# All eight output-gate projections moved between the keys and the mLSTM values, with the gate scan beside them

## The chip, the cores and the metric

The kernel runs on one core of a Trainium2 chip. The metric is the device time in microseconds of one execution. Before the change three runs took 955.58, 956.19 and 957.11 us; the median is 956.19 us.

## The reference, cut to what matters

One decoder layer on 512 tokens of width 1024, all in float32. One RMS-normalised input `h` is multiplied by one wide matrix; its column blocks feed a chunkwise mLSTM (4 heads), a sliding-window attention (16 query heads on 4 key heads), and two branch gates. The parts that the change touches:

```
proj = h @ w_in[i]
qk_ml, v_ml, o_ml, if_pre, q_sw, k_sw, v_sw, g_a, g_b = jnp.split(proj, split_idx, axis=-1)
...
gates = (if_pre + b_if[i]).astype(jnp.float32)
ig = gates[..., :ML_HEADS]
lf = jax.nn.log_sigmoid(gates[..., ML_HEADS:])
h_ml = mlstm_chunkwise(q_ml, k_ml, v_ml.reshape(B, S, ML_HEADS, ML_DV), ig, lf)
h_ml = h_ml * lax.rsqrt(jnp.mean(h_ml * h_ml, axis=-1, keepdims=True) + EPS)
y_a = jax.nn.sigmoid(o_ml) * h_ml
y_b = swa_with_sinks(q_sw, k_sw, v_sw, sinks[i])
merged = jax.nn.sigmoid(g_a) * (y_a @ w_branch_a[i]) + jax.nn.sigmoid(g_b) * (y_b @ w_branch_b[i])
```

After that come an output projection, a squared-ReLU MLP, a gated per-layer embedding and a final norm, none of which the change touches.

## The kernel before, in words

Every float32 operand of a matrix product is split into a high part and a low part: ScalarE casts the high part (L134), VectorE subtracts it from the source (L135), and TensorE takes three products per pair (high by high, high by low, low by high). A projection to 128 output channels (`proj_T`, L288) is thus 24 products of 128x128 by 128x512 into one PSUM bank. Its weights come as one 512 KB transfer into a ring of four raw buffers (`wr`), and are split into rings of four buffers (`wh`, `wl`); the cast for a fifth weight waits until TensorE has finished with the first.

PSUM has three tags: `g` (two banks, for projections), `t` (two banks, for transposes and small results; the key projections use it too), `a` (two pairs of banks). Instructions of one engine run in the order in which they stand; that order comes from a scheduler that works when the kernel is built, so it need not be the order of the source.

The stages that matter here, in time:

- Norm, and the projection of the SWA values and the gate pre-activations (`gt`), up to about 31 us.
- The two key projections (L297 to L307). The keys are wanted on both halves of the partitions, so each result is cast and subtracted four times, in half-height pieces of 64x512 (`kk` at L304, `kl` at L305).
- The sums of `h` over token halves (`h_sum`, L326) and their splits (`h_split`, tiles `hS`), which the next two stages use as operands of a Strassen-Winograd scheme (`seven`, L350: seven products in place of eight). VectorE also forms sums of the raw weights in place (L359, L360, L365, L367).
- The mLSTM values (`vml`), 168 products of 512 columns; then the two branch gates (`gate_proj`), whose sigmoids go to DRAM.
- Four of the eight output-gate projections (`o_proj`, L482; sigmoid at L485), written to DRAM through POOL's queue (L491).
- The gate scan (L494 to L537): transposes of `gt`, log-sigmoid by Exp and Ln with their table loads on ScalarE, three kinds of VectorE instructions on four partitions (the scans at L509 and L512 among them), the maxima `em` by another Exp, and 14 little transposes into `gc`.
- SWA: query projections (`q_proj`, each in half-height pieces), scores, softmax, outputs, with the mLSTM's query and key projections in between; then the mLSTM itself with the second branch's projections between.
- The loop over `ya` (L744 to L753): for each of eight blocks four transposes of the normed mLSTM output, a multiply by the norm gain and the output gate (`sy`, L752), and a split into `ya`. The gates of blocks 0 to 3 are read back from DRAM in pairs (`gate_of`, two buffers of the tag `pT`), those of blocks 4 to 7 are projected inside this loop.
- The first branch's projections (L757), which need all eight blocks of `ya`, then the rest of the layer.

SyncE's queue issues all weight loads, in order, each waiting for its buffer.

Of the kernel before, what the change touches and what calls it, by code (L numbers as in the profile page):

```python
# [36 lines left out]
def block_kernel(  # L37
# [29 lines left out]
    nc = tc.nc  # L67
    V, A, G, T = nc.vector, nc.scalar, nc.gpsimd, nc.tensor


    def pool(stack, name, **kw):
        return stack.enter_context(tc.tile_pool(name=name, bufs=1, reuse_waits="tile", **kw))
# [7 lines left out]
    c1 = pool(st_s, "c1", side="right")  # L80
# [5 lines left out]
    def nm(s):  # L86
        n_names[0] += 1
        return f"{s}_{n_names[0]}"


    def ps_g():
        return pp.tile([P, 512], F32, tag="g", bufs=2, name=nm("psg"))

    def ps_t():
        return pp.tile([P, 512], F32, tag="t", bufs=2, name=nm("pst"))
# [9 lines left out]
    def act_f(n="f"):  # L105
        return ap.tile([P, 512], F32, tag="act", bufs=NACT, name=nm(n))
# [21 lines left out]
    def r32(t):  # L128
        return t.bitcast(F32)

    def split(dst, src, scale=None):

        if scale is None:
            A.copy(dst[0], src)  # L134
            V.tensor_sub(dst[1], src, r32(dst[0]))  # L135
        else:
            A.activation(dst[0], src, AF.Copy, scale=scale)
            V.scalar_tensor_tensor(dst[1], src, scale, r32(dst[0]), ALU.mult, ALU.subtract)
# [7 lines left out]
    def load_w(src, n, dims, raw=None):  # L146

        if raw is None:
            raw = load_raw(src, n)
        parts = [wp.tile([P, 1056], F32R, tag=t, bufs=WB, name=nm(t))[:, :n] for t in ("wh", "wl")]  # L150
        split(parts, raw[:, :n])
        return [q.rearrange("p (k c) -> p k c", k=dims) for q in parts]
# [5 lines left out]
    last_mm = [None]  # L158
# [17 lines left out]
    def mm_T(ps, w, acts, first=True, last=True):  # L176

        ops = []
        for k in range(len(acts)):
            ops += pairs([q[:, k, :] for q in w], acts[k])  # L180
        chain(ps, ops, first, last)
# [11 lines left out]
    ident = cp.tile([P, P], F32, name="ident")  # L193
# [5 lines left out]
    zeros4 = c1.tile([4, P], F32, name="zeros4")  # L199
# [10 lines left out]
    sel_f = c1.tile([4, 4, P], F32, name="sel_f")  # L210
# [45 lines left out]
    gt = c1.tile([P, NT, 8], F32, name="gt")  # L256
    h2, hT = big_hl("h")
    hf = []
    for m in range(NT):
# [4 lines left out]
        for c in range(2):  # L264
            o = slice(c * 512, (c + 1) * 512)
# [4 lines left out]
        for kq in range(2):  # L270
            ps = ps_t()
# [8 lines left out]
        ps = ps_g()  # L280
        for c in range(2):
            mm_tok(ps[:, :264], wv[c], hT[c * 4 : c * 4 + 4], m, first=c == 0, last=c == 1)
        t = sp.tile([P, 256], F32, tag="vs", bufs=4, name=nm("vs"))
# [4 lines left out]
    def proj_T(wd, i, bank=ps_g):  # L288
        ps = bank()
        mm_T(ps, load_w(wd[i], KT * P, KT), hT)  # L290
        return ps
# [3 lines left out]
    HALF = [slice(0, 64), slice(64, 128)]  # L295
    kk, kl = [], []
    for i in range(2):  # L297
        ps = proj_T(w_ksw, i, ps_t)
        both = [act_r("kk"), act_r("kk")]
        low = [act_r("kl"), act_r("kl")]  # L300
        for ab in range(2):
            s = HALF[ab]
            for o in (s, HALF[1 - ab]):
                A.copy(both[ab][o, :], ps[s, :])  # L304
                V.tensor_sub(low[ab][o, :], ps[s, :], r32(both[ab][o, :]))  # L305
        kk.append(both)
        kl.append(low)  # L307

    vm = []
    for m in range(NT):  # L310
        t = tk("vm").rearrange("p (h d) -> p h d", h=NH)
# [21 lines left out]
    def h_split(t):  # L333
        f = []
        for kh in range(2):
            hl = [q.rearrange("p (k c) -> p k c", k=2) for q in act_hl("hS")]
            split(hl, t[:, 2 * kh : 2 * kh + 2, :])
            f += [[q[:, k, :] for q in hl] for k in range(2)]
        return f
# [5 lines left out]
    s4, _ = h_sum("s4", hf_part(1, 2), s2h, ALU.subtract)  # L345
    s3, _ = h_sum("s3", hf_part(1, 1), hf_part(2, 1), ALU.subtract)
    S3 = h_split(s3)
    S4 = h_split(s4)

    def seven(form, prod, X, Y, Z, b, post):  # L350

# [23 lines left out]
        for i in n:  # L375
            prod(Z, S4, form(b22[i]), i, False, True)
        post("c12", Z)
# [37 lines left out]
    vml()  # L415


    dp = pool(ctx, "dp", space=bass.MemoryType.DRAM)

    def gate_proj(wd):  # L420

# [49 lines left out]
    def gate_of(put, i):  # L471

        if i % 2 == 0:
            loaded[0] = sp.tile([P, 2, 512], F32, tag="pT", bufs=2, name=nm("gl"))
            nc.sync.dma_start(out=loaded[0], in_=put[i // 2])
        return loaded[0][:, i % 2, :]

    gbd = gate_proj(w_gb)
    gad = gate_proj(w_ga)
    scan_at = last_mm[0].ins  # L480

    def o_proj(i):  # L482
        ps = proj_T(w_o, i)
        t = act_f("sgo")
        A.activation(t, ps, AF.Sigmoid)  # L485
        return t


    god = [dp.tile([P, 2, 512], F32, name=nm("god")) for _ in range(2)]
    for i in range(4):  # L490
        nc.gpsimd.dma_start(out=god[i // 2][:, i % 2, :], in_=o_proj(i))  # L491


    pgi, pgf = ps_t(), ps_t()  # L494
    with tc.issue_after(scan_at):
        for m in range(NT):
            T.transpose(pgi[:4, m * P : (m + 1) * P], gt[:, m, :4], ident)
            T.transpose(pgf[:4, m * P : (m + 1) * P], gt[:, m, 4:], ident)
    ig = act_f("ig")[:4, :]
    fg = act_f("fg")[:4, :]  # L500
    V.tensor_copy(ig, pgi[:4, :])
    V.tensor_copy(fg, pgf[:4, :])
    lf = act_f("lf")[:4, :]
    V.scalar_tensor_tensor(lf, fg, -1.0, fg, ALU.mult, ALU.max)
    A.activation(lf, lf, AF.Exp, scale=-1.0)
    A.activation(lf, lf, AF.Ln, bias=1.0)
    V.scalar_tensor_tensor(lf, fg, 0.0, lf, ALU.min, ALU.subtract)
    mst = act_f("mst")[:4, :]
    V.tensor_tensor_scan(mst, lf, ig, 0.0, ALU.add, ALU.max)  # L509
    fl = act_f("fl")[:4, :]  # L510
    for c in range(NT):
        V.tensor_tensor_scan(fl[:, c * P : (c + 1) * P], lf[:, c * P : (c + 1) * P], zeros4, 0.0, ALU.add, ALU.add)  # L512
    rr = act_f("rr")[:4, :]
    V.tensor_sub(rr, fl, mst)
    sel = c1.tile([4, 4, P], F32R, name="sel")
    A.copy(sel, sel_f)
    rrh = [c1.tile([4, 512], F32R, name=f"rrh{i}") for i in range(2)]
    split(rrh, rr)
    gg = [act_f("gg")[:4, :] for _ in range(NT)]
    for t in range(NT):  # L520
        sl = slice(t * P, (t + 1) * P)
        V.tensor_sub(gg[t][:, sl], ig[:, sl], fl[:, sl])
        if t:
            V.tensor_scalar_add(gg[t][:, : t * P], gg[t - 1][:, : t * P], fl[:, t * P - 1 : t * P])
    em = act_f("em")[:4, :]
    A.activation(em, mst, AF.Exp, scale=-1.0)
    pgc = ps_t()
    for t in range(NT):
        for s in range(t + 1):
            c = (t * NT + s) * 4  # L530
            T.transpose(pgc[:, c : c + 4], gg[t][:, s * P : (s + 1) * P], ident[:4, :4])
        c = (NT * NT + t) * 4
        T.transpose(pgc[:, c : c + 4], em[:, t * P : (t + 1) * P], ident[:4, :4])
    gc = c1.tile([P, NT * NT + NT, 4], F32, name="gc")
    for t in range(NT):
        V.tensor_copy(gc[:, t * NT : t * NT + t + 1, :], pgc[:, t * NT * 4 : (t * NT + t + 1) * 4].rearrange("p (a b) -> p a b", b=4))
    V.tensor_copy(gc[:, NT * NT :, :], pgc[:, NT * NT * 4 : (NT * NT + NT) * 4].rearrange("p (a b) -> p a b", b=4))  # L537

    qs = {}

# [203 lines left out]
    ya = [act_hl("ya") for _ in range(8)]  # L744
    for i in range(8):
        h, dv = i // 2, i % 2
        so = gate_of(god, i) if i < 4 else o_proj(i)
        sg = act_f("sy")
        pt = ps_t()
        for t in range(NT):  # L750
            T.transpose(pt[:, t * P : (t + 1) * P], h_of(h, t)[:, dv * P : (dv + 1) * P], ident)
        V.scalar_tensor_tensor(sg, pt, gml[:, i : i + 1], so, ALU.mult, ALU.mult)  # L752
        split(ya[i], sg)  # L753
# [3 lines left out]
    for i in range(8):  # L757
        ps = ps_g()
# [34 lines left out]
    for nh in range(2):  # L793
        if nh == 0:
            a, b = pair(), pair()
            pv = [a[:, 0, :], a[:, 1, :], b[:, 0, :], b[:, 1, :]]
        else:
            a = pair()
# [5 lines left out]
        for m in range(NT):  # L804
            o = xk[m][:, nh * 512 : (nh + 1) * 512]
# [12 lines left out]

    A21, A11, A22, A12, S1, S2, S3, S4 = range(8)
    rB = mp.tile([P, 512], F32, name="rB")  # L820
# [23 lines left out]
    def up(q, uf):  # L844
        fs = None
        for f in range(8):
# [8 lines left out]
            if f % 2:  # L855
                V.tensor_add(fs[:, S1, :], fs[:, A21, :], fs[:, A22, :])
                V.tensor_sub(fs[:, S3, :], fs[:, A11, :], fs[:, A21, :])
                V.tensor_sub(fs[:, S2, :], fs[:, S1, :], fs[:, A11, :])
                V.tensor_sub(fs[:, S4, :], fs[:, A12, :], fs[:, S2, :])  # L859
                hl = [np_.tile([P, 7 * 256], F32R, tag="uf", bufs=8, name=nm("uf")) for _ in range(2)]  # L860
# [3 lines left out]
    def down(q, uf):  # L864
# [51 lines left out]
        for kh in range(2):  # L916
            prod(Z, S4, form(b22[kh]), kh, False, True)
        acc(Z, 1, 1)
# [69 lines left out]
    a, b = pair(), pair()  # L988
# [8 lines left out]
    for m in range(NT):  # L997
        for o in (0, 256):
            ps = ps_g()[:, :256]
# [98 lines left out]
```

## Time and profile before

| | |
|---|---|
| median of three runs | 956.19 us (955.58 to 957.11) |
| the profiled execution | 955.62 us, its span 953.9 us |
| TensorE busy | 909.8 us, 95% of the span |
| VectorE busy | 645.6 us, 68% |
| ScalarE busy | 461.4 us, 48% |
| DMA | 97.31 MB, mean 102 GB/s |
| mean granted TensorE clock | 0.989 |

The span runs from the first to the last instruction of one execution; the device time of that execution is 1.7 us longer. Busy time of TensorE is modelled for pipelined products, so a stage is best read by the distance from one product's start to the next one's, and by the idle time that the trace puts before an instruction. PE stands for TensorE, DVE for VectorE, ACT for ScalarE, POOL for GpSimd, SP for SyncE. "L162" is the line from which every product of a split operand is issued, so tile names tell the stages apart: `pst` with `wh` are the keys, `psa` and `psg` with `hS` or `h` the values, gates and other projections.

### The profile page before, as it was taken

The page shows a single profiled execution, that of the slowest core. Times are in us where ns is not written, and L with a number is a line of the kernel's source. Part 1 is how long each engine was busy: PE and PEld are TensorE (multiplying, and loading weights), DVE is VectorE, ACT ScalarE, POOL GpSimd, SP SyncE. Part 2 cuts the span into 40 slices and gives each one's busy share as a digit, 9 for nine tenths or more (in the row PEclk, how much of TensorE's full clock was granted, in tenths as well). Part 3 has the DMA queues.
Part 4 walks back from the last instruction along what each step waited for, and adds up shares of the span by engine and source line. Part 5 has one row for each costly group of instructions (what it writes and reads, how often), then busy time and mean ns, then how long its engine had stood idle before and what let it go on. Part 6 is the DMA issues. An engine that isn't in the chain of part 4 may idle for free.

```text
span 953.9 us, 11756 instructions
## 1 busy us (share of the span) xinstructions
PE 909.8 (95%) x4498; PEld 743.4 (78%) x4498; DVE 645.6 (68%) x992; ACT 461.4 (48%) x772; POOL 33.4 (3%) x49
## 2 busy tenths in 40 slices
PE   7959999989999999999999999999999999989995
PEld 5748999867877667788888887888788788867785
DVE  6877877454887874455654578757967885797365
ACT  7543544343685675544222545334434533435546
POOL 1000000000000000000210000000000000000032
PEclk9979999998999999999999999999999999999999
DMA  7221333631111131243352520631252063104202
GB/s 277 79 89 45 133 142 128 217 114 64 45 67 45 66 111 66 67 133 111 133 198 89 199 89 1 199 117 37 89 185 79 1 197 112 45 1 155 67 1 88
DMA packets 28602, 97.31 MB, mean 102 GB/s; under 512 B 3969, under 2 KB 4481, under 8 KB 28546
## 3 DMA queue, kind: packets, MB, share of 16 engines
q1 hardware_dynamic: 27074, 91.32, 27.9%
q0 software_dynamic: 1472, 5.24, 1.6%
q8 instruction: 35, 0.57, 0.2%
q14 instruction: 21, 0.17, 0.1%
HBM read 89.21 MB, written 7.34 MB: 101 GB/s over the span
## 4 chain that ended last, share of the span: by engine, by line
PE 83%; DVE 7%; ACT 5%; DMA 2%; issue 2%; SPq 0%; DVEq 0%; ACTq 0%
PE psg L162 49%; PE psp L162 20%; PE psa L162 6%; DVE wl L135 2%; PE pst L700 2%; ACT wh L134 2%; PE pst L627 1%; PE pst L162 1%; PE pst L690 1%; DVE uf L135 1%; PE psa L619 1%; ACT lm L601 1%; PE psa L582 1%; DMA xt<-in_x 1%; PE psa L583 1%
## 5 line engine op out<-in xcount | busy, mean ns | idle before, releaser
L135 DVE TENSOR_TENSOR wl<-wr,wh 128x1024 fp32r<-128x1024 f32 (+1 forms) x136 | 174.7, 1287 | 109.6 <-ACT wh L134 105.0
L134 ACT CAST wh<-wr 128x1024 fp32r<-128x1024 f32 (+1 forms) x136 | 142.5, 1050 | 218.5 <-PE psg L162 106.6
L162 PE MATMUL psg<-x,wh 128*128 128x512 f32 x512 | 160.1, 393 | 0.0
L162 PE MATMUL psp<-wh,uf 128*128 128x512 f32 x448 | 141.1, 394 | 2.0 <-DVE uf L135 2.0
L162 PE MATMUL psg<-h,wh 128*128 128x512 f32 x384 | 124.3, 403 | 0.6 <-DVE qs L547 0.6
L162 PEld LDWEIGHTS psg<-x,wh 128*128 128x128 f32 x512 | 96.1, 188 | 21.2
L162 PEld LDWEIGHTS psp<-wh,uf 128*128 128x128 f32 x448 | 83.8, 188 | 23.3 <-DVE uf L135 3.7
L162 PE MATMUL psg<-x,wl 128*128 128x512 f32 x256 | 100.5, 393 | 0.0
L162 PE MATMUL psp<-wl,uf 128*128 128x512 f32 x224 | 88.0, 393 | 2.0 <-DVE wl L135 2.0
L162 PEld LDWEIGHTS psg<-h,wh 128*128 128x128 f32 x384 | 71.6, 191 | 20.9 <-issue 6.6
L134 ACT CAST wh<-wd 128x1024 fp32r<-128x1024 f32 x44 | 45.9, 1051 | 70.5 <-PE psp L162 34.0
L162 PE MATMUL psg<-h,wl 128*128 128x512 f32 x192 | 76.5, 398 | 0.0
L135 DVE TENSOR_TENSOR wl<-wd,wh 128x1024 fp32r<-128x1024 f32 x44 | 53.0, 1220 | 8.8 <-ACT wh L134 8.5
L162 PEld LDWEIGHTS psg<-x,wl 128*128 128x128 f32 x256 | 48.1, 188 | 10.7
L162 PEld LDWEIGHTS psp<-wl,uf 128*128 128x128 f32 x224 | 42.1, 188 | 11.9 <-DVE wl L135 2.4
L135 DVE TENSOR_TENSOR uf<-F,uf 128x1792 fp32r<-128x1792 f32 x16 | 32.4, 2023 | 21.8 <-ACT uf L134 21.8
L162 PEld LDWEIGHTS psg<-h,wl 128*128 128x128 f32 x192 | 36.6, 191 | 9.5 <-issue 1.6
L162 PE MATMUL psg<-yb,wh 128*128 128x512 f32 x128 | 42.5, 408 | 0.0
L850 DVE SCALAR_TENSOR_TENSOR rt<-psg,rB 128x512 f32<-128x512 f32 x32 | 22.0, 688 | 27.8 <-PE psg L162 27.8
L162 PE MATMUL psg<-ya,wh 128*128 128x512 f32 x128 | 39.9, 393 | 0.0
L134 ACT CAST uf<-F 128x1792 fp32r<-128x1792 f32 x16 | 27.1, 1695 | 24.7 <-DVE F L859 24.7
L162 PE MATMUL psa<-h,wh 128*128 128x256 f32 x192 | 35.1, 284 | 0.2 <-ACT p L449 0.2
(267 smaller groups left out, 1684.3 us busy)
## 6 DMA issues: line engine op xcount, KB each, us to landing
wr<-in_w_up SPq DMA_DIRECT2D x32, 512.0 KB, 4.2
wd<-in_w_down SPq DMA_DIRECT2D x24, 512.0 KB, 4.4
gd<-gr POOLq DMA_DIRECT2D x8, 512.0 KB, 3.0
wr<-in_w_o SPq DMA_DIRECT2D x8, 512.0 KB, 3.3
wr<-in_w_qsw SPq DMA_DIRECT2D x8, 512.0 KB, 4.3
wr<-in_w_qkml SPq DMA_DIRECT2D x8, 512.0 KB, 3.2
wr<-in_w_b SPq DMA_DIRECT2D x8, 512.0 KB, 3.2
gl<-gd SPq DMA_DIRECT2D x8, 512.0 KB, 3.3
```

Of the source, the lines that this page charges most:

```text
L134: A.copy(dst[0], src)
L135: V.tensor_sub(dst[1], src, r32(dst[0]))
L162: last_mm[0] = T.matmul(ps, l, r, start=first and i == 0, stop=last and i == len(ops) - 1, skip_group_check=parts)
L582: T.matmul(o, q[:, n * P : (n + 1) * P], kk[kp][ab][:, k0 : k0 + 256], start=True, stop=False)
L583: T.matmul(o, q[:, n * P : (n + 1) * P], kl[kp][ab][:, k0 : k0 + 256], start=False, stop=True)
L601: A.activation(lm3[:, g, :], lm3[:, g, :], AF.Exp, bias=nmx[:, g : g + 1], accum_out=sm[:, g : g + 1])
L619: T.transpose(pt[:, c : c + P], lm3[ab][:, g, j * P : (j + 1) * P], ident)
L627: T.matmul(o[HALF[ab], :], vs[n + 1 - nk + j][:, c : c + 64], pTs[j][:, ab * 512 : (ab + 1) * 512], start=j == 0, stop=j == nk - 1,)
L690: T.matmul(psc[:, n0:], qk[4 + h][:, n0 : n0 + P], qk[h][:, n0:], start=True, stop=True)
L700: T.matmul(pn[:, : DV + 1], wT[s][:, t * P : (t + 1) * P], vm[s][:, h, :], start=s == 0, stop=s == t)
L850: V.scalar_tensor_tensor(a, ps, 0.0, rB, ALU.max, ALU.mult)
```

## The change

All eight output-gate projections and the whole scan now stand between the key projections and the mLSTM values. Projections 0 and 1 come after the scan's source lines, 2 to 4 after the sums of `h`, then the 14 little transposes into `gc`, then 5 to 7. Every sigmoid is written to DRAM (four tiles `god` of two blocks each) and all eight are read back in the loop over `ya`, which no longer projects anything. The key pieces are cast and subtracted once each; their copies on the other half of the partitions are made by eight SBUF-to-SBUF transfers on SyncE's queue. No arithmetic is added or left out.

```diff
         for ab in range(2):
-            s = HALF[ab]
-            for o in (s, HALF[1 - ab]):
-                A.copy(both[ab][o, :], ps[s, :])
-                V.tensor_sub(low[ab][o, :], ps[s, :], r32(both[ab][o, :]))
+            s, o = HALF[ab], HALF[1 - ab]
+            A.copy(both[ab][s, :], ps[s, :])
+            V.tensor_sub(low[ab][s, :], ps[s, :], r32(both[ab][s, :]))
+            nc.sync.dma_start(out=r32(both[ab])[o, :], in_=r32(both[ab])[s, :])
+            nc.sync.dma_start(out=r32(low[ab])[o, :], in_=r32(low[ab])[s, :])
...
+    god = [dp.tile([P, 2, 512], F32, name=nm("god")) for _ in range(4)]
+    def o_proj(i):
+        ps = proj_T(w_o, i)
+        t = act_f("sgo")
+        A.activation(t, ps, AF.Sigmoid)
+        nc.gpsimd.dma_start(out=god[i // 2][:, i % 2, :], in_=t)
+    pgi, pgf = ps_t(), ps_t()
+    for m in range(NT):
+        T.transpose(pgi[:4, m * P : (m + 1) * P], gt[:, m, :4], ident)
+        T.transpose(pgf[:4, m * P : (m + 1) * P], gt[:, m, 4:], ident)
...
+    em = act_f("em")[:4, :]
+    A.activation(em, mst, AF.Exp, scale=-1.0)
+    o_proj(0)
+    o_proj(1)
...
     S3 = h_split(s3)
     S4 = h_split(s4)
+    for i in range(2, 5):
+        o_proj(i)
+    pgc = ps_t()
+    with tc.issue_after(last_mm[0].ins):
+        for t in range(NT):
...
+    for i in range(5, 8):
+        o_proj(i)
...
-    scan_at = last_mm[0].ins
-    god = [dp.tile([P, 2, 512], F32, name=nm("god")) for _ in range(2)]
-    for i in range(4):
-        nc.gpsimd.dma_start(out=god[i // 2][:, i % 2, :], in_=o_proj(i))
-    pgi, pgf = ps_t(), ps_t()
-    with tc.issue_after(scan_at):
...
     for i in range(8):
         h, dv = i // 2, i % 2
-        so = gate_of(god, i) if i < 4 else o_proj(i)
+        so = gate_of(god, i)
```

More of the change, by code (lines that the diff above doesn't have):

```diff
@@ L301, in block_kernel @@
         for ab in range(2):
-            s = HALF[ab]
-            for o in (s, HALF[1 - ab]):
-                A.copy(both[ab][o, :], ps[s, :])
-                V.tensor_sub(low[ab][o, :], ps[s, :], r32(both[ab][o, :]))
+            s, o = HALF[ab], HALF[1 - ab]
[3 more added lines that the diff above has]
+            nc.sync.dma_start(out=r32(low[ab])[o, :], in_=r32(low[ab])[s, :])
         kk.append(both)
         kl.append(low)
+    dp = pool(ctx, "dp", space=bass.MemoryType.DRAM)
+    god = [dp.tile([P, 2, 512], F32, name=nm("god")) for _ in range(4)]
[8 more added lines that the diff above has]
+        T.transpose(pgf[:4, m * P : (m + 1) * P], gt[:, m, 4:], ident)
+    ig = act_f("ig")[:4, :]
+    fg = act_f("fg")[:4, :]
+    V.tensor_copy(ig, pgi[:4, :])
+    V.tensor_copy(fg, pgf[:4, :])
+    lf = act_f("lf")[:4, :]
+    V.scalar_tensor_tensor(lf, fg, -1.0, fg, ALU.mult, ALU.max)
+    A.activation(lf, lf, AF.Exp, scale=-1.0)
+    A.activation(lf, lf, AF.Ln, bias=1.0)
+    V.scalar_tensor_tensor(lf, fg, 0.0, lf, ALU.min, ALU.subtract)
+    mst = act_f("mst")[:4, :]
+    V.tensor_tensor_scan(mst, lf, ig, 0.0, ALU.add, ALU.max)
+    fl = act_f("fl")[:4, :]
+    for c in range(NT):
+        V.tensor_tensor_scan(fl[:, c * P : (c + 1) * P], lf[:, c * P : (c + 1) * P], zeros4, 0.0, ALU.add, ALU.add)
+    rr = act_f("rr")[:4, :]
+    V.tensor_sub(rr, fl, mst)
+    sel = c1.tile([4, 4, P], F32R, name="sel")
+    A.copy(sel, sel_f)
+    rrh = [c1.tile([4, 512], F32R, name=f"rrh{i}") for i in range(2)]
+    split(rrh, rr)
+    gg = [act_f("gg")[:4, :] for _ in range(NT)]
+    for t in range(NT):
+        sl = slice(t * P, (t + 1) * P)
+        V.tensor_sub(gg[t][:, sl], ig[:, sl], fl[:, sl])
+        if t:
+            V.tensor_scalar_add(gg[t][:, : t * P], gg[t - 1][:, : t * P], fl[:, t * P - 1 : t * P])
+    em = act_f("em")[:4, :]
+    A.activation(em, mst, AF.Exp, scale=-1.0)
+    o_proj(0)
+    o_proj(1)
     vm = []
@@ L348, in block_kernel @@
     S4 = h_split(s4)
+    for i in range(2, 5):
+        o_proj(i)
+    pgc = ps_t()
+    with tc.issue_after(last_mm[0].ins):
+        for t in range(NT):
+            for s in range(t + 1):
+                c = (t * NT + s) * 4
+                T.transpose(pgc[:, c : c + 4], gg[t][:, s * P : (s + 1) * P], ident[:4, :4])
+            c = (NT * NT + t) * 4
+            T.transpose(pgc[:, c : c + 4], em[:, t * P : (t + 1) * P], ident[:4, :4])
+    gc = c1.tile([P, NT * NT + NT, 4], F32, name="gc")
+    for t in range(NT):
+        V.tensor_copy(gc[:, t * NT : t * NT + t + 1, :], pgc[:, t * NT * 4 : (t * NT + t + 1) * 4].rearrange("p (a b) -> p a b", b=4))
+    V.tensor_copy(gc[:, NT * NT :, :], pgc[:, NT * NT * 4 : (NT * NT + NT) * 4].rearrange("p (a b) -> p a b", b=4))
+    for i in range(5, 8):
+        o_proj(i)
     def seven(form, prod, X, Y, Z, b, post):
@@ L415, in block_kernel @@
     vml()
-    dp = pool(ctx, "dp", space=bass.MemoryType.DRAM)
     def gate_proj(wd):
@@ L479, in block_kernel @@
     gad = gate_proj(w_ga)
-    scan_at = last_mm[0].ins
[L482 to L486, printed above, removed]
-    god = [dp.tile([P, 2, 512], F32, name=nm("god")) for _ in range(2)]
-    for i in range(4):
-        nc.gpsimd.dma_start(out=god[i // 2][:, i % 2, :], in_=o_proj(i))
-    pgi, pgf = ps_t(), ps_t()
-    with tc.issue_after(scan_at):
-        for m in range(NT):
-            T.transpose(pgi[:4, m * P : (m + 1) * P], gt[:, m, :4], ident)
-            T.transpose(pgf[:4, m * P : (m + 1) * P], gt[:, m, 4:], ident)
@@ L499, in block_kernel @@
[L499 to L536, printed above, removed]
@@ L537, in block_kernel @@
-    V.tensor_copy(gc[:, NT * NT :, :], pgc[:, NT * NT * 4 : (NT * NT + NT) * 4].rearrange("p (a b) -> p a b", b=4))
     qs = {}
```

## The prediction

> **What bounds the kernel now.** I read the page's totals first, then TensorE's waits in the stages that the change touches, then these stages as windows, then the timelines of TensorE, ScalarE and VectorE inside them.
>
> ```profile
> span 953.9 us, 11756 instructions
> PEclk9979999998999999999999999999999999999999
> PE 83%; DVE 7%; ACT 5%; DMA 2%; issue 2%; SPq 0%; DVEq 0%; ACTq 0%
> ```
>
> TensorE sets the time nearly everywhere: 83% of the chain that ended last. What can be won is where it stands still or runs at a lower clock. The row of the granted clock, 40 slices of 23.85 us, dips twice: to 0.7 in the third (48 to 72 us) and to 0.8 in the tenth (215 to 238). TensorE's waits in the first of these places (sum in us, count, longest):
>
> ```profile
> PE psa L162 <- ACT p L403: 7.1, 1, 7.1
> PE psg L162 <- ACT hS L134: 2.0, 1, 2.0
> PE psg L162 <- DVE hS L135: 1.1, 1, 1.1
> ```
>
> These 10.2 us lie in the mLSTM values: TensorE has no operand while VectorE and ScalarE do the key pieces, the weight sums and the splits of h's sums. The second halt is at the scan, seen in TensorE's timeline (start, duration, instruction, idle before it):
>
> ```profile
> 198.12 0.28 PE L497 MATMUL pst<-ident,gt 128*4 128x128 f32 x1
> 198.92 0.71 PE L162 MATMUL psg<-h,wh 128*128 128x512 f32 x2
> ...
> 214.11 0.22 PE L533 MATMUL pst<-ident,em 4*128 4x4 f32 x1 [2.85 <-ACT em L526]
> 214.88 0.20 PE L533 MATMUL pst<-ident,em 4*128 4x4 f32 x1
> 216.35 0.58 PE L582 MATMUL psa<-kk,qs 128*128 128x256 f32 x1 [1.28 <-DVE qs L547]
> ```
>
> Both stages and the start of the `ya` loop as windows (length, busy time of PE, PEld, DVE, ACT, POOL, granted clock, DMA share, GB/s), with one SWA window for later; and the chain's rows that give the pace of a product:
>
> ```profile
> 41.25:94.55 53.30, 43.06 (x171) 33.86 (x169) 39.27 (x47) 23.72 (x31) 0.37 (x4) 0.90 0.18 60
> 198.12:231.08 32.96, 27.52 (x122) 21.67 (x121) 17.21 (x33) 14.31 (x19) 0.54 (x1) 0.90 0.21 72
> 419.36:445.25 25.89, 25.89 (x129) 21.05 (x128) 17.26 (x30) 12.46 (x18) 0.00 (x0) 1.00 0.44 142
> 300.00:315.00 15.00, 13.40 (x79) 10.52 (x77) 12.75 (x43) 12.01 (x37) 0.00 (x0) 1.00 0.11 36
> ```
>
> ```profile
> 30.59 10.82 PE pst L162 x47
> 65.07 7.50 PE psa L162 x24
> 72.57 5.56 PE psg L162 x24
> 176.18 22.11 PE psg L162 x96
> ```
>
> At full clock a product costs 22.11 / 96 = 0.230 us. The values are 168 products, 38.7 us of work; they stand between the end of the keys (30.59 + 10.82 = 41.41, which overlaps the next start by 0.16) and 94.55, a window of 53.3 us. So **14.6 us are lost there**: 10.2 idle, the rest at a low clock (24 products took 7.50 us right after the 7.1 us halt, 5.56 later: 1.94 us for one such halt). In the scan's window four query projections (96 products, 22.1), eight transposes (0.8, from 198.12 to 198.92), fourteen (about 0.9, from 214.11) and one score pair (0.23, two products of half the columns) are 24.0 of 32.96 us: **8.9 us lost**. The `ya` window holds 96 products and 32 transposes without a halt; 25.89 - 22.1 = 3.8 us is the transposes.
>
> **The change part by part.** TensorE's work stays the same to within nothing, it moves. So the sum is: what is lost now at these two places goes, and what the new order loses is added. I walk the new order of each engine with the durations above and below.
>
> *The new first stage.* After the keys TensorE has 192 products of `o_proj` in front of the values, 44 us, in which the sums and splits of h are done. The old 14.6 go. But ScalarE's new order matters: the cast for projection 4's weight, Exp, Ln, the cast for projection 5's weight, the cast `rrh`, `em`, and only then the sigmoid of projection 0. Projection 2 writes the bank which that sigmoid frees, as `g` has two banks. The scan's own pieces today (ScalarE, then VectorE):
>
> ```profile
> 199.04 0.59 ACT L485 ACTIVATE sgo<-psg 128x512 f32<-128x512 f32 x1
> 199.65 1.28 ACT L505 ACT_TABLE_LOAD   x1
> ...
> 204.27 0.63 ACT L506 ACTIVATE lf<-lf 4x512 f32<-4x512 f32 x1
> ...
> 209.87 0.62 ACT L134 CAST rrh<-rr 4x512 fp32r<-4x512 f32 x1 [4.02 <-DVE rr L514]
> 211.07 1.04 ACT L134 CAST wh<-wr 128x1024 fp32r<-128x1024 f32 x1 [0.59 <-PE psg L162]
> ```
>
> ```profile
> 204.93 0.68 DVE L507 SCALAR_TENSOR_TENSOR lf<-fg,lf 4x512 f32<-4x512 f32 x1 [2.64 <-ACT lf L506]
> 205.65 1.21 DVE L509 TENSOR_TENSOR_SCAN mst<-lf,ig 4x512 f32<-4x512 f32 x1
> 206.78 1.33 DVE L512 TENSOR_TENSOR_SCAN fl<-lf,zeros 4x128 f32<-4x128 f32 x4
> ...
> 209.16 0.67 DVE L514 TENSOR_TENSOR rr<-fl,mst 4x512 f32<-4x512 f32 x1
> ```
>
> Projection 0 starts at 41.25 with eight transposes (0.9) among its 24 products (5.5) and ends at about 48.0; projection 1 ends at 53.5. Projection 4's cast has to wait for the end of projection 0, as its buffer is the fifth: 48.0 + 1.0. Exp with its load, Ln with its load: 2 x (1.28 + 0.63) = 3.8, to 52.85. VectorE: 0.7 + 1.1 + 1.3 + 0.7 to `rr`, to 56.65. ScalarE: `rrh` 0.62, load 1.28, `em` 0.63, load 1.28, sigmoid 0.59, to 61.1. TensorE could have gone on at 53.5, so it stands **7.7 us**, and pays the 1.94 of low clock behind it: **+9.6**. Its bounds: 0, if the sigmoid came before the chain, and 12, if the half-height key pieces hold the second set of transposes by 1 to 2 us more (its bank is freed by the keys' last subtraction, 41.4 plus a weight's cast and subtraction that stand ahead, 2.3, plus two subtractions and a cast of key pieces, 2.0: 45.7, within 0.1 us of where TensorE gets to it). Queued behind the chain on ScalarE are also the casts of `hS` and of projections 6 and 7; after 61 us TensorE has six projections, 33 us, to cover them, and I find no second halt. The values then run on 8 weight buffers that are ready, as they do today from 65 us on.
>
> [...]
>
> *The scan's old place.* The gates are followed straight by the query projections; the 8.9 go. The scan's products `sel`, `rrh`, `gc` are wanted only in the mLSTM, long after. What is late next: ScalarE now needs one Exp load ahead of the first softmax, 1.28 us, beside query and key projections. I take 0, bounds 0 and 1.3.
>
> *The keys' copies.* Four casts and four subtractions of a half-height piece fewer, eight transfers more:
>
> ```profile
> 39.73 0.69 DVE L305 TENSOR_TENSOR kl<-pst,kk 64x512 fp32r<-64x512 f32 x1
> god<-sgo POOLq DMA_DIRECT2D x4, 256.0 KB, 2.6
> gl<-god SPq DMA_DIRECT2D x2, 512.0 KB, 3.2
> ```
>
> The time saved on VectorE, 4 x 0.6, lies inside the old 14.6. On SyncE's queue the transfers wait for the pieces until 45.7, ahead of the loads for projections 6, 7 and the values, whose casts come, by the walk above, at 69, 74 and 80; the copies are first read in SWA (today at 216). Nearest row 2.6 us: 0 on the path; bounds 0 and, if each of the eight held the queue for its whole 2.6 us, 21 us from 45.7, to 66.7: still ahead of 69.
>
> *The `ya` loop.* This is where the old cover goes: projections 4 to 7 ran while VectorE made `ya`. VectorE and ScalarE there today:
>
> ```profile
> 422.25 2.18 DVE L721 TENSOR_SCALAR hs<-hs,rs 128x256 f32<-128x256 f32 x8
> 424.35 0.68 DVE L135 TENSOR_TENSOR ya<-sy,ya 128x512 fp32r<-128x512 f32 x1
> 424.95 0.74 DVE L752 SCALAR_TENSOR_TENSOR sy<-pst,gml,gl 128x512 f32<-128x512 f32 x1
> 426.38 0.69 DVE L135 TENSOR_TENSOR ya<-sy,ya 128x512 fp32r<-128x512 f32 x1 [0.68 <-ACT ya L134]
> 426.99 0.74 DVE L752 SCALAR_TENSOR_TENSOR sy<-pst,gml,gl 128x512 f32<-128x512 f32 x1
> ```
>
> The new order of VectorE is the same up to here, then goes on in this pattern: multiply, wait for ScalarE's cast, subtract; 426.99 - 424.95 = 2.04 us a block. TensorE's new order puts the first two projections of the first branch among the transposes, six products for each block of `ya`; that is 1.38 + 0.47 = 1.85 us a block. So VectorE sets the pace. In the old time axis: block 0 complete at 425.0; block 1's multiply at 424.95, block 7's at 424.95 + 6 x 2.04 = 437.2, its low part at 439.3, four more products, 440.4. Unhindered, 48 products and the transposes would be 11.05 + 3.8 from 419.36: 434.2. **+6.2**, and 0.3 for the bank of the third projection, which the multiply of the first frees: **+6.5**. The reads of `god` wait for a buffer two pairs back, 3.2 us each; block 4's is issued when block 1's multiply is done (425.7, landing 428.9) and wanted at 431: hidden, with 2 us to spare. Bounds: 3.1 (only the wait for block 0) and 16.0 (the first rival).
>
> Sum: -14.6 - 8.9 + 9.6 + 6.5 = **-7.4**. The profiled execution took 955.62 us, 1.7 more than its span, so 948.2; it lies 0.6 below the median of the runs, so I say **948.8**.
>
> **The rivals.** *Half clock through the `ya` loop* (slower). TensorE waits some 3 us for block 0 (its last free work, the transposes of blocks 1 and 2, ends by 421.9) and then a little for each block. If these small halts kept the clock at half, a block would cost 6 x 0.46 + 0.94 = 3.7 us in place of 2.04: from 425.0 four products (1.8) and seven blocks (25.9), less three blocks' transposes done before (2.8), give 449.9 for 440.4, 9.5 more. That is +16.0 there, and the kernel at 958.3. It decides once the clock stays at half for longer than the first two blocks, because up to there VectorE's pace hides it. For it: the values' stage has clock 0.90 with halts of 2.0 and 1.1 us. Against: the SWA window from 300 has TensorE idle for 1.6 of 15 us, the 9 to 10% of this loop, at 1.00; and a block at half clock needs 3.7 us of every 2.04, which keeps TensorE busy, so it should rise. [...]
>
> *No halt behind the scan.* If the scan's chain ended before projection 1 (the change then does all that its place allows), the 9.6 go: 939.2. Against: the chain from the first transposes to `em` lasts from 198.1 to 214.1 now, 16 us, and projection 1 ends 12 us after it begins.
>
> *SWA ordered worse.* The scheduler gives SWA's output products 6, 3 and 4 products less cover behind the copies they wait for: 13 x 0.23 = 3.0 us at the most, 951.8. Against: VectorE is the busy one there and catches up in between.
>
> **How the numbers follow.** The forecast has 0.70, with a range of its own of 946 to 951 (1 us either way at the halt, 1.5 at `ya` and SWA). Worse SWA 0.12, half clock 0.10, no halt 0.06, the rest unknown. With the ends of the unknown costs I take 943.5 to 955. A measurement of this kernel tells 0.2% from no change, 1.9 us: faster 0.84 (forecast, SWA, no halt less a little), same 0.06, slower 0.10.
>
> **What would show it.** TensorE should halt once between 50 and 62 us, before the third `o_proj`, for 7 to 8 us, released by ScalarE's sigmoid; no halt of over 1 us from there to the query projections; the values at 5.5 us for 24 products; no halt between gates and queries; in the `ya` loop `sy` every 2.0 us and TensorE waiting on VectorE's `ya`. I am wrong if the halt is under 4 or over 11 us, or if the granted clock in the `ya` loop stays near half.

## The result, and the profile after

The changed kernel takes 954.40 us (median of 14 runs, 953.12 to 956.90); the kernel before, on the same chip and beside it, took 958.16 us (14 runs, 954.52 to 961.53). The ratio is 0.996, with a 95% interval from 0.9947 to 0.9974: 3.8 us faster, between 2.5 and 5.1. The forecast was 7.4 us faster, 948.8 us. The direction was right and the gain about half. The profiled execution took 953.72 us. Its page begins so (span, granted clock in 40 slices, shares of the chain):

```profile
span 952.0 us, 11780 instructions
PEclk9989999999999999998999999999999999999999
PE 70%; DVE 4%; ACT 3%; issue 1%; DMA 0%; DVEq 0%; SPq 0%; ACTq 0%
```

The dip to 0.8 in the tenth slice, where the scan stood, is gone; there is a dip at the `ya` loop now (19th slice), and the low clock early in the kernel is one slice of 0.8 rather than 0.7. The two longest of TensorE's waits in the stages that the change touches (total, count, longest):

```profile
PE psg L162 <- ACT sgo L317: 7.7, 1, 7.7
PE psg L162 <- DVE ya L135: 2.6, 1, 2.6
```

The first is the halt behind the scan's chain. In TensorE's timeline:

```profile
54.69 0.40 PE L162 MATMUL psg<-h,wl 128*128 128x512 f32 x1
62.77 1.22 PE L162 MATMUL psg<-h,wh 128*128 128x512 f32 x2 [7.69 <-ACT sgo L317]
63.79 0.63 PE L162 MATMUL psg<-h,wl 128*128 128x512 f32 x1
...
67.45 0.40 PE L162 MATMUL psg<-h,wl 128*128 128x512 f32 x1
```

The 1.22 us for two products, where 0.62 is usual, is the low clock behind it: granted 0.50 from 60.38 to 67.21 us, 1.00 behind that. ScalarE's timeline tells what TensorE waited for:

```profile
53.65 0.63 ACT L332 ACTIVATE lf<-lf 4x512 f32<-4x512 f32 x1
54.88 1.04 ACT L134 CAST wh<-wr 128x1024 fp32r<-128x1024 f32 x1 [0.60 <-PE psg L162]
58.25 0.62 ACT L134 CAST rrh<-rr 4x512 fp32r<-4x512 f32 x1 [2.33 <-DVE rr L340]
58.89 1.28 ACT L352 ACT_TABLE_LOAD   x1
60.18 0.63 ACT L352 ACTIVATE em<-mst 4x512 f32<-4x512 f32 x1
60.83 1.28 ACT L317 ACT_TABLE_LOAD   x1
62.12 1.08 ACT L317 ACTIVATE sgo<-psg 128x512 f32<-128x512 f32 x2
```

Projection 0 was finished long before; its sigmoid, which frees the bank for projection 2, is last in this queue.

To see where the time went I cut both executions at the same four places: end of the keys, first gate product, first score product (a place that lies between different work in the two kernels, so the second and third rows are read together), first transpose for `ya`, first product of the output projection `w_out`. Columns as in the windows of the prediction. Before, then after:

```profile
41.63:94.55 52.92, 42.68 (x170) 33.53 (x168) 38.89 (x47) 23.57 (x31) 0.37 (x4) 0.90 0.18 60
94.55:216.35 121.80, 116.81 (x839) 108.86 (x837) 81.70 (x108) 57.16 (x69) 6.61 (x12) 1.00 0.42 147
216.35:419.19 202.84, 200.12 (x944) 151.66 (x945) 132.63 (x374) 123.35 (x336) 0.00 (x0) 0.99 0.20 68
419.19:489.30 70.11, 70.11 (x322) 57.18 (x321) 45.27 (x54) 25.92 (x35) 9.00 (x7) 1.00 0.37 125
```

```profile
42.93:138.16 95.23, 87.53 (x382) 70.18 (x381) 58.35 (x76) 41.89 (x52) 4.79 (x12) 0.96 0.26 91
138.16:242.55 104.39, 103.53 (x770) 98.50 (x769) 73.45 (x87) 47.33 (x58) 4.26 (x8) 1.00 0.42 147
242.55:430.70 188.15, 186.30 (x897) 140.81 (x896) 127.34 (x368) 121.09 (x331) 0.00 (x0) 1.00 0.21 71
430.70:486.14 55.44, 51.66 (x225) 41.44 (x224) 37.01 (x50) 18.27 (x26) 10.80 (x7) 0.94 0.42 140
```

The four lengths add to 447.67 us before and 443.21 after: 4.5 us won in the region that the change touches. What lies outside it, the same code in both, took 506.2 us before (953.9 - 447.67) and 508.8 after (952.0 - 443.21): 2.6 us more. One more profile of each kernel (below) settles which of the two is a property of the kernel.

### The profile page after: what moved, and what is told of

Read it like the earlier page. It is cut to its first block, busy times and chain, and to the rows that moved or that the text cites. A ratio compares the mean times of both kernels' runs of the same rounds, so it can differ in the third digit from the quotient of the medians.

```text
span 952.0 us, 11780 instructions
## 1 busy us (share of the span) xinstructions
PE 911.4 (96%) x4498; PEld 744.5 (78%) x4498; DVE 638.5 (67%) x988; ACT 458.0 (48%) x767; POOL 38.0 (4%) x53
## 4 chain that ended last, share of the span: by engine, by line
PE 70%; DVE 4%; ACT 3%; issue 1%; DMA 0%; DVEq 0%; SPq 0%; ACTq 0%
PE psg L162 41%; PE psp L162 20%; PE pst L708 2%; PE pst L635 1%; PE psa L627 1%; DVE wl L135 1%; PE pst L698 1%; PE psa L162 1%; PE psa L590 1%; DVE uf L135 1%; ACT wh L134 1%; PE psa L591 1%; DVE xk L983 1%; DMA ptok<-in_p 0%; DVE prod L981 0%
## 5 line engine op out<-in xcount | busy, mean ns | idle before, releaser
L135 DVE TENSOR_TENSOR wl<-wr,wh 128x1024 fp32r<-128x1024 f32 (+1 forms) x136 | 170.4, 1255 | 113.7 <-ACT wh L134 113.6
L162 PEld LDWEIGHTS psg<-x,wl 128*128 128x128 f32 x256 | 48.2, 188 | 10.6
L162 PE MATMUL psg<-ya,wh 128*128 128x512 f32 x128 | 42.3, 411 | 3.0 <-DVE ya L135 2.6
```

Of the source, the lines that this page charges most:

```text
L162: last_mm[0] = T.matmul(ps, l, r, start=first and i == 0, stop=last and i == len(ops) - 1, skip_group_check=parts)
```

## The experiments

In all of them I give the time, the ratio to runs of the kernel before on the same chip, and the length of this region, called R.

**The same two kernels again.** No edit.

> The kernel before once more. The profiled execution after the change starts its key projections 1.29 us later than the one before (31.72 against 30.43), though no instruction ahead of them differs, and loses another 1.26 us behind the first branch, where nothing differs either. Theory A, both are chance (when the first inputs land, where a clock window falls): in this execution the keys start somewhere from 30 to 32, and the down projections run slow in some executions of either kernel. Theory B, the change causes the late start: the keys start at 30.4 +- 0.2 here, and at 31.7 +- 0.2 in every kernel with the new order.

> The changed kernel once more. Theory A (chance): keys' start anywhere from 30 to 32; span between 948 and 954. Theory B (caused by the change): keys start at 31.7 +- 0.2. Under both the halt before the third output-gate projection is 7.7 us, the branch gates lose 0.8 us at one bank, and the loop over ya takes 22 us from its first transposes to the third product of the first branch.

Before: 960.13 us, R 447.97. After: 952.71 us, R 442.28. So R repeats within 1 us and the change is worth 4.5 and 5.7 in it, 5.1 in the mean. What lies outside was 510.4 (span 958.4) and 508.7 (951.0): the order of the two kernels is reversed. The keys began at 31.27 us here in the kernel before and at 31.08 in the changed one, and between 30.4 and 32.3 in the thirteen profiles of this study, in no relation to the kernel; that they start 1.3 us later in the changed kernel's first profile is chance, and not the change. The rest of the scatter is at two places near the end, in code that no kernel here alters; they are told of in the last section.

**Two more banks behind the halt.**

```
-        ps = proj_T(w_o, i)
+        ps = proj_T(w_o, i, (lambda: ps_a()[:, :512]) if i in (2, 3) else ps_g)
```

> Only the PSUM banks of output-gate projections 2 and 3 differ: they take halves of the two double banks, idle at that point, so the third projection no longer waits for the sigmoid behind the scan's chain. Theory: that halt is 7.7 us plus about 2.1 us of low clock behind it, and nothing else waits there: TensorE has no halt between keys and values and the kernel is 9 to 10 us faster than the changed one, about 1.4% faster than the one before. Rival: the casts of h's splits and of weights 6 and 7 are late as well behind the chain, so the halt moves to projection 4 or 6 and only 2 to 5 us are won.

945.31 us, ratio 0.9861 (0.9842 to 0.988), R 432.85. TensorE's timeline at the same place, and the first stage as a window:

```profile
64.85 0.40 PE L162 MATMUL psa<-h,wl 128*128 128x512 f32 x1
65.09 0.62 PE L162 MATMUL psg<-h,wh 128*128 128x512 f32 x2
```

```profile
42.04:127.30 85.26, 85.25 (x382) 68.77 (x381) 58.19 (x76) 41.57 (x52) 4.78 (x12) 1.00 0.32 102
```

TensorE doesn't stand still in 85 us, as the theory said; projection 4 takes its bank at 65.09 with no wait. The stage is 10.0 us shorter than the changed kernel's 95.23, with the same instructions: that is the price of the halt, 7.69 idle and 2.3 of low clock.

**Two projections back in the `ya` loop.** Six early, 6 and 7 in the loop's last two turns:

```
+        if i >= 6:
+            return t
...
-    for i in range(5, 8):
+    for i in range(5, 6):
...
-        so = gate_of(god, i)
+        so = gate_of(god, i) if i < 6 else o_proj(i)
```

> Only output-gate projections 6 and 7 go back into the loop over ya; six stay early. Theory: the loop lost 7.4 us because VectorE and ScalarE hand each block back and forth every 2.04 us while TensorE had nothing else; 11 us of projections cover nearly all of it, so the stretch from the first transposes to the end of the first branch's first two projections costs 0.5 to 1.5 us over its work, and the kernel is 6 to 7 us faster than the changed one, about 1.1% faster than the one before. Rival: the loss comes from the reads of the gates from DRAM and from the low clock, not from cover; then the loop still loses 4 us or more.

950.66 us, ratio 0.9918 (0.99 to 0.9935): 3.7 less than the changed kernel, short of what the theory said. From the first transpose to `w_out` it takes 62.51 us; 48 products at 0.230 are 11.05 of it, so 51.5 remain, where the kernel before, less its four projections (22.1), needs 48.0 and the changed kernel 55.2 (mean of two). So 3.5 of the 7.2 us lost stay, which is neither the theory's 0.5 to 1.5 nor the rival's 4 or more, and the wait has a new name:

```profile
435.98 0.66 PE L761 MATMUL pst<-ident,hs 128*128 128x128 f32 x4 [0.59 <-DVE sy L762]
438.72 0.73 PE L162 MATMUL psg<-ya,wh 128*128 128x512 f32 x2 [2.08 <-ACT sgo L317]
```

ScalarE has cast `ya` up to then and loads the sigmoid's table (1.28 us) only at 436.78; the bank is free at 438.7. The cover was there, but its result was fetched late.

**The scan alone back at its old place.** All eight projections stay early; the scan and its small transposes stand behind the gate projections again, as in the kernel before.

> The change with the scan alone back at its old place behind the gate projections (all eight o_proj stay early). Theory (the halt before the third o_proj is the scan's chain on ScalarE, 7.7 us and about 2 of low clock; the scan's old place costs 8.9): no halt of over 1 us between keys and gates, 33 us between gates and first score pair instead of 24, so about 1.5 us faster than the changed kernel: 952 to 954, ratio 0.993 to 0.996. Rival (the halt comes from h's sums or the keys' transfers): the halt stays at 6 us or more and 9 us are lost again at the scan: 962 or more.

952.9 us, ratio 0.9946 (0.9928 to 0.9964), R 440.73, 2.0 shorter than the changed kernel's mean. The first stage takes 83.07 us without a halt, so h's sums and the keys' transfers have no part in it. At the old place the old waits return, in TensorE's timeline:

```profile
223.42 0.22 PE L542 MATMUL pst<-ident,em 4*128 4x4 f32 x1 [2.85 <-ACT em L535]
...
225.66 0.58 PE L591 MATMUL psa<-kk,qs 128*128 128x256 f32 x1 [1.28 <-DVE qs L556]
```

Moved without the two banks, the scan thus costs a little more at its new place (95.27 - 83.07 = 12.2 us, its 22 transposes among them) than it frees at the old one (302.5 against 292.3 us from gates to `ya`: 10.2).

**The keys' copies by casts and subtractions again.**

```
-            nc.sync.dma_start(out=r32(both[ab])[o, :], in_=r32(both[ab])[s, :])
-            nc.sync.dma_start(out=r32(low[ab])[o, :], in_=r32(low[ab])[s, :])
...
+            for o in (s, HALF[1 - ab]):
+                A.copy(both[ab][o, :], ps[s, :])
+                V.tensor_sub(low[ab][o, :], ps[s, :], r32(both[ab][o, :]))
```

> The change with the keys' second copies made by casts and subtractions again, no transfers. Theory (the transfers cost and win nothing, since the chain behind ScalarE has slack up to the end of projection 0): within 1 us of the changed kernel, 953.5 to 955.5, and the halt before the third o_proj still 7 to 9 us. Rival (the copies by transfer are what keeps the first stage short): 2 us or more slower than the changed kernel, the halt over 9.5 us. Second rival (transfers hold SyncE's queue and cost): 2 us or more faster.

956.25 us, ratio 0.999 (0.9973 to 1.0007), R 445.25: 2.5 us longer than the changed kernel in R, 1.9 by the medians. My theory fell; the halt is the first rival's, though the median stays just short of its 2 us.

```profile
65.65 1.22 PE L162 MATMUL psg<-h,wh 128*128 128x512 f32 x2 [11.62 <-ACT sgo L316]
```

The halt grows by 3.9 us. ScalarE and VectorE have four casts and four subtractions more, up to 50.9. Counted from the end of the keys (41.99 here, 42.93 in the changed kernel), the second set of transposes comes 2.7 us later (49.02 for 47.28) and Exp 1.6 us later (52.35 for 51.71), so there was no slack ahead of the chain. Then ScalarE's next weight cast, which stood behind Ln, stands in front of it and waits for TensorE:

```profile
54.17 1.04 ACT L134 CAST wh<-wr 128x1024 fp32r<-128x1024 f32 x1 [1.19 <-PE psg L162]
```

With that Ln comes 3.8 us later (56.53 for 53.65). Some 1.6 us are thus the copies' own and 2.2 the new order in ScalarE's queue; no run has the copies with the old order.

**The same in the bank version.** The same edit, and projections 2 and 3 in the `a` banks.

> The bank version (945.3) with the keys' second copies by casts and subtractions again. Casts in place of transfers made the halt before the third o_proj 11.6 us instead of 7.7. Theory (the copies delay the scan's chain on ScalarE by some 4 us, and that counts only where TensorE waits for the chain): with two more banks TensorE reaches projection 4 at about 65 us, as the chain would now end, so no halt of over 1 us and within 1 us of the bank version: 944.5 to 946.5. Rival (the transfers shorten work that counts by itself): 2 us or more slower than the bank version, 947.3 or more.

945.97 us, ratio 0.9862 (0.9836 to 0.9888), R 433.93, 1.1 longer than with transfers. One wait of 1.56 us is left at projection 4, for the chain's sigmoid again, where none of over 1 us was expected. So what the transfers win is time that TensorE waits for the chain: 2.5 us of R with the two banks of `g`, 1.1 with two more.

**A faster pace in `ya`.** On the bank version, the low-part subtraction of a block is issued behind the next block's multiply, so that VectorE need not wait for ScalarE's cast:

```
-        split(ya[i], sg)
+        A.copy(ya[i][0], sg)
+        if i:
+            V.tensor_sub(ya[i - 1][1], sy_last, r32(ya[i - 1][0]))
+        sy_last = sg
+    V.tensor_sub(ya[7][1], sy_last, r32(ya[7][0]))
```

> The bank version (945.3) with the low-part subtraction of each block of ya issued behind the next block's multiply, so VectorE's pace falls from 2.04 to about 1.45 us a block and TensorE's 1.85 sets it. Theory (of the 7.4 us lost in the ya loop about 3 are VectorE's pace, 3 the wait for block 0, which stays): 3 us faster than the bank version, 941.5 to 943.5, sy every 1.85 us. Rival (the loss is the wait for block 0 and its low clock alone): within 1 us of the bank version, 944.5 to 946.

941.66 us, ratio 0.9836 (0.981 to 0.9862), R 429.36, 3.5 shorter. VectorE's timeline:

```profile
426.35 0.74 DVE L760 SCALAR_TENSOR_TENSOR sy<-pst,gml,gl 128x512 f32<-128x512 f32 x1
...
427.61 0.74 DVE L760 SCALAR_TENSOR_TENSOR sy<-pst,gml,gl 128x512 f32<-128x512 f32 x1
...
431.68 0.75 DVE L760 SCALAR_TENSOR_TENSOR sy<-pst,gml,gl 128x512 f32<-128x512 f32 x1 [1.47 <-DMA gl<-god]
```

1.26 us a block instead of 2.04, until the read of `god` is late. From the transposes to `w_out` it is 52.2 us: 3 of the 7.2 us lost go, 4.2 stay. The edit does more than quicken the pace: the multiply of block 1 now stands ahead of the scaling of `hs` (2.18 us), TensorE's wait for block 0 is 1.68 us instead of 2.64, and the clock is full all through the loop (products 0.23 us apart between the waits), where the bank version's profile has it at half for 6.8 us (0.94 in the mean over its 55.35 us). How the 3 us divide between these isn't separated.

**Bank and cover together.**

> Bank and cover together (projections 2 and 3 in halves of the a banks; projections 6 and 7 back in the ya loop). Theory (two losses at two places, they add): 945.3 less the 3.7 that cover alone won, 940.5 to 942.5, ratio 0.980 to 0.983. Rival (with no halt in front, six projections no longer cover h's sums and splits, and what cover wins is lost before the values): 943.5 or more, with a new halt of 2 us or more between 60 and 90 us.

939.97 us, ratio 0.9819 (0.9791 to 0.9847), R 428.85: the two gains add (the sum of the single ones gives 941.6, and 429.6 for R). No halt of over 1 us stands before the values. The wait for `sgo` in the loop is there as before, 2.07 us.

**The two late projections spread.** Projection 6 ahead of the loop, 7 behind its fourth block, so that the table load has time; then the same with VectorE's faster pace.

```
+    late = {6: o_proj(6)}
     ya = [act_hl("ya") for _ in range(8)]
     for i in range(8):
+        if i == 4:
+            late[7] = o_proj(7)
...
-        so = gate_of(god, i)
+        so = gate_of(god, i) if i < 6 else late[i]
```

> The bank version with projection 6 ahead of the ya loop and projection 7 behind its fourth block, instead of both in the loop's last two turns. Theory (what cover still lost, 3.5 us, is the first sigmoid with its table load behind the casts of ya; placed early it has time): 2 to 3 us faster than bank with cover, 937 to 938.5, no wait of over 1 us between the transposes of ya and w_out. Rival (VectorE's pace of 2.04 us a block shows again, since one projection covers less behind block 4): within 1 us of bank with cover, 939.5 to 941.

> The same with the low-part subtractions issued one block later (VectorE at about 1.45 us a block). Theory (two projections cover the wait for block 0, TensorE's 1.85 us a block sets the rest): the loop's loss falls from 3.5 to under 1 us, 936.5 to 938. If the spread alone already takes all, within 0.7 us of it; if VectorE's pace still shows there, 1 to 3 us faster than it.

936.44 us, ratio 0.9767 (0.9744 to 0.979), R 426.24; and 936.48 us, ratio 0.9762 (0.9736 to 0.9788), R 426.06. TensorE's timeline where cover waited, and the stage as a window, both without the faster pace:

```profile
421.50 0.60 PE L764 MATMUL pst<-ident,hs 128*128 128x128 f32 x4
421.85 0.71 PE L162 MATMUL psg<-ya,wh 128*128 128x512 f32 x2
```

```profile
414.04:467.81 53.77, 53.77 (x249) 43.52 (x248) 34.98 (x39) 20.64 (x28) 10.73 (x7) 1.00 0.45 143
```

Busy for all of 53.77 us at full clock; less the 24 products of projection 7 (5.5) that is 48.2, against 48.0 in the kernel before. The spread takes the whole loss, and the faster pace then adds nothing. It is the best version that I have: 22.6 us under the kernel before by the medians of the runs beside it (959.01), and 18 under the changed kernel's 954.40, which comes from another set of runs.

## Why the prediction was half right

The mechanism was right: TensorE halts where the walk put the halt, and for its reason. What failed is the size of the sum. Of its terms the new first stage was the most mis-sized: -14.6 + 9.6 = -5.0 us forecast, -3.3 measured. The `ya` loop follows, +6.5 forecast and +7.2 measured. And the sum was subtracted from 956.2 us, where the kernel before takes 958.16 by the median of 14 runs.

The terms of the sum, each against the profiles (two of each kernel, their means):

| Term | forecast | measured | worked out |
|---|---|---|---|
| lost before the gates goes | -14.6 | -14.0 | 52.67 us less 168 products x 0.230 |
| halt behind the scan's chain | +9.6 | +10.0 | 95.23 less 85.26 of the bank version |
| rest of the first stage | 0 | +0.7 | 85.26 less 360 products x 0.2303 and 1.7 for transposes |
| the scan's old place | -8.9 | -9.0 | see below |
| `ya` loop without cover | +6.5 | +7.2 | 55.2 less 48.0 |
| sum | -7.4 | -5.1 | |

*Halt behind the scan.* Place, cause and size were right. It was forecast from 53.5 to 61.1; it came from 55.1 to 62.77, 7.69 us, released by the sigmoid as the walk of ScalarE's queue had it. The forecast's own figures give 61.1 - 53.5 = 7.6 and not 7.7; that 7.7 meets the measurement to a hundredth is luck. That the halt goes with two more banks, and goes with the scan moved away, shows the cause. The low clock behind it cost 2.3 where 1.94 was taken.

*The first stage.* The bank version, without a halt, takes 85.26 us; the version without a scan there takes 83.07, which is 360 products at 0.231. The 22 small transposes are thus 2.2 us between the projections; I had counted 1.7 for them at the old place and no more than that at the new. Also the old loss was 14.2 and 13.7 us when the window begins at the end of the keys, not 14.6 from a window that began 0.38 us early. With the halt's 0.4 these make the stage 1.7 us worse than forecast: -3.3 in place of -5.0.

*The scan's old place.* From gates to `ya`, before: 302.5 and 303.4 us once 22.1 for four projections are taken off; after: 292.5 and 292.0. That is 10.7 less, of which 1.7 is the transposes that only moved: 9.0, with 8.9 forecast. Inside the gates stands a small halt that the walk had not:

```profile
204.55 0.50 PE L162 MATMUL psa<-h,wh 128*128 128x256 f32 x2 [0.84 <-ACT p L515]
```

It is 0.84 us here and 0.30 in the second profile, under the 1 us that the prediction named. Its cause wasn't tried.

*The `ya` loop.* VectorE's `sy` comes every 2.04 us and TensorE waits for block 0, as walked; with the low parts issued a block later 3 us of the loss go, with the two projections well placed nearly all. TensorE's and VectorE's timelines after:

```profile
433.21 0.73 PE L162 MATMUL psg<-ya,wh 128*128 128x512 f32 x2
436.58 0.80 PE L162 MATMUL psg<-ya,wh 128*128 128x512 f32 x1 [2.64 <-DVE ya L135]
...
439.16 1.63 PE L162 MATMUL psg<-ya,wh 128*128 128x512 f32 x3
...
442.57 1.00 PE L162 MATMUL psg<-ya,wh 128*128 128x512 f32 x3
```

```profile
436.44 0.74 DVE L760 SCALAR_TENSOR_TENSOR sy<-pst,gml,gl 128x512 f32<-128x512 f32 x1
...
438.48 0.74 DVE L760 SCALAR_TENSOR_TENSOR sy<-pst,gml,gl 128x512 f32<-128x512 f32 x1
...
442.90 0.75 DVE L760 SCALAR_TENSOR_TENSOR sy<-pst,gml,gl 128x512 f32<-128x512 f32 x1 [0.27 <-PE pst L759]
```

The half-clock rival showed itself for about 6 us and no longer: the granted clock is 0.50 from 435.85 to 442.68 us, as it was from 215.51 to 222.34 at the scan's old place before, and 1.00 behind it; three products take 1.63 us at 439.16, then 1.00 at 442.57, where the clock rises between them. I had let VectorE's pace hide all of the low clock; the last row shows that it doesn't, since VectorE waits 0.27 us for a transpose that came late. That is a part of the 0.7: where the clock is at half for 6.8 us (this profile, the bank version and the scan moved back, 0.94 in the mean) the stretch from the transposes to `w_out` takes 55.1 to 55.4 us, where it is for 3.4 us (the changed kernel's second profile, 0.97 in the mean, and the two with the old key copies) 54.9 to 55.0. The rest isn't separated.

*The keys' copies.* The time was put at nothing on the path, because the walk counted it inside the old 14.6. That holds only for the walk with the fewer key pieces: with the old copies the halt is 11.62 us. In this kernel, where TensorE waits for the chain, the transfers with the order that comes with them are worth 2.5 us; the prediction named no such price.

*SWA ordered worse* did not come. From the scores to `ya` TensorE's idle time is 1.85 and 1.89 us in the two profiles after, and 2.72 and 2.75 in the two before; its one wait of over 1 us there, 1.6 us for a copy (`pT`), is the same in all four. Nor is anything missing from the 9.0 above.

*The time it was summed against.* The profiled execution shown before the change took 506.2 us outside the region. In thirteen profiles of this study, whose code there is the same, it took 506.2 to 510.6, and the one shown was the shortest. The three runs shown (median 956.19) lay below the median of all 14 (958.16). Of the 5.6 us from 948.8 to 954.4, 2.0 are this base, 2.3 are the terms above, and 1.3 lie between R's 5.1 and the 3.8 of the medians. R rests on two profiles of each kernel, and 5.1 is the upper end of the ratio's interval (2.5 to 5.1); what makes up the 1.3 stays open.

## What to carry to other kernels

Before work is moved in front of a long chain on another engine, walk that engine's queue for the instruction that frees a bank, and count the banks: here two more took a halt of 10 us away with a one-line edit, and moving the scan without them gained nothing by itself. Cover that is taken from a loop should be left where its wait is, and the result fetched early, with its table load: two projections of eight were enough, once they stood right. A sum against one profiled execution inherits that execution's luck at its own halts, so read them for the low clock before taking its time as base.

## What the runs showed of the hardware

The same halt is followed by a low clock in some executions and not in others. Late in the MLP's down projection TensorE waits 1.98 to 2.00 us for a weight's low part, in every profile. The kernel before in its two profiles: first the products at this halt, of the one and the other, then windows of 3.41 us at it and at a later halt, again of the one and the other (TensorE's busy time behind the length, granted clock in the third column from the end):

```profile
853.98 0.50 PE L162 MATMUL psp<-wl,uf 128*128 128x512 f32 x1 [1.98 <-DVE wl L135]
854.32 0.62 PE L162 MATMUL psp<-wh,uf 128*128 128x512 f32 x2
```

```profile
855.14 0.73 PE L162 MATMUL psp<-wl,uf 128*128 128x512 f32 x1 [1.98 <-DVE wl L135]
855.68 1.05 PE L162 MATMUL psp<-wh,uf 128*128 128x512 f32 x2
```

```profile
850.39:853.80 3.41, 1.61 (x7) 0.95 (x6) 3.18 (x3) 0.00 (x0) 0.00 (x0) 1.00 0.00 0
853.80:857.22 3.42, 3.24 (x14) 2.70 (x15) 3.42 (x4) 0.00 (x0) 0.00 (x0) 1.00 0.00 0
932.31:935.73 3.42, 1.67 (x14) 1.67 (x15) 2.61 (x8) 2.57 (x5) 0.12 (x1) 1.00 0.41 153
935.73:939.14 3.41, 3.41 (x32) 3.41 (x30) 2.37 (x5) 3.27 (x5) 1.36 (x2) 1.00 0.00 0
```

```profile
851.82:855.24 3.42, 1.44 (x7) 0.85 (x5) 3.20 (x4) 0.00 (x0) 0.00 (x0) 1.00 0.00 0
855.24:858.65 3.41, 3.41 (x8) 2.65 (x9) 3.25 (x3) 0.04 (x1) 0.00 (x0) 0.50 0.00 0
933.74:937.16 3.42, 0.30 (x3) 0.24 (x3) 1.31 (x4) 3.38 (x5) 0.54 (x1) 1.00 0.12 44
937.16:940.57 3.41, 3.41 (x18) 3.41 (x18) 2.68 (x6) 2.45 (x7) 1.47 (x2) 0.50 0.29 109
```

From this halt to the next small one it is 23.3 us in six of the thirteen profiles and 24.8 to 24.9 in seven, and nothing between. At a halt of 3.1 us near the end the stretch behind takes 11.7 us in four and 13.1 to 13.2 in nine. The kernel before and the bank version with the old key copies drew the short case at both places: 506.2 and 506.3 us outside the region; the five that drew the long one at both took 509.5 to 510.6. So the halt of 2 us cost 1.6 us more here, or nothing.

Which of the two comes is not set by the kernel: the rows above are two executions of the same one. In the first, the window with 1.61 us of products in 3.41 and the one with 1.67 in 3.42 are followed by 1.00; in the second, 1.44 us in 3.42 and 0.30 in 3.42 are followed by 0.50 for 3.41 us each, in which TensorE is busy throughout. Half the work of 3.41 us is 1.7, an estimate that meets the 1.6 measured. In the first profile of the kernel before, the granted clock up to the last product was 0.50 from 51.67 to 55.09, from 61.91 to 68.74 and from 215.51 to 222.34 us; in that of the changed kernel from 60.38 to 67.21, from 435.85 to 442.68 and from 852.28 to 855.69. In the 3.41 us ahead of these falls TensorE was busy for 1.42, 0.00 and 0.96 us, and for 0.00, 1.38 and 1.42. What decides whether the clock falls was not shown: no run varies this halt alone.
